# A function table set loaded by hand ahead of each logarithm group of a mixer on ScalarE

## The chip, the cores and the metric

The kernel runs on one core of one Trainium2 chip. The metric is the device time of one execution in microseconds (us); the time given for a kernel is the median of several executions. A core has five engines that run their own queues in order and wait for each other through semaphores: TensorE (PE in the profile, with its weight loads as PEld), VectorE (DVE), ScalarE (ACT), GpSimd (POOL) and SyncE (SP), which here issues most of the transfers.

## What is computed

A decoder trunk of two layers over 1024 tokens of width 1024, float32. The first layer mixes by eight retention heads and eight RWKV-7 heads side by side, the second by sliding-window attention; each is followed by a SwiGLU feed-forward, and a last RMS norm ends the trunk. What matters here is the first layer's mixer, cut to its lines with a nonlinear function:

```python
n = rms_norm(h, norm1_g[0]); z = n @ w_in                      # rsqrt
q, k, v, g = split(z_ret); o = chunk_retention(rotary(q), rotary(k), v)
ret_out = head_group_norm(o) * silu(g)                          # rsqrt, silu
w_log = -softplus(-(w0 + tanh(wl) @ w_up)) - 0.5
decay = exp(-exp(w_log));  a = sigmoid(a0 + al @ a_up)
gate = sigmoid(gl) @ g_up
kk = kkf / maximum(norm(kkf), 1e-12)                            # rsqrt
y = rwkv7_scan(r, decay, k * (1 + (a - 1) * k_a), v, -kk, kk * a)
rwkv_out = (head_group_norm(y) * ln_g + ln_b + bonus) * gate    # rsqrt
out = concat(ret_out, rwkv_out) @ w_out
```

## The kernel before

The tokens are worked in two halves of 512, features on the 128 partitions. Matmuls of the projections are split into a high and a low part and run as three products. ScalarE has no reciprocal square root in use: each `rsqrt` is a logarithm followed by an exponential with scale -0.5, two instructions on ScalarE. Sigmoid, silu and the decay are written with Tanh and Exp in the mixer; the feed-forward uses Silu.

An activation on ScalarE needs its function in the table set that is loaded. Unless the kernel loads a set by name, a load is put in ahead of an activation whose function is not in the set that stands; it appears in the profile as `ACT_TABLE_LOAD` with the line of that activation.

The mixer (`mixer0`) writes its instructions through a planner (`Plan`): chains of work, written as Python generators, and projection jobs (`step`, the line of all mixer matmuls is L240) are drawn in the order of an estimated time that the planner keeps. Its chains are

- `first_norm` and `second_norm`: the RMS factor of each half. `factor` (L479 logarithm, L480 exponential) belongs to the first, L566 and L567 to the second.
- `pair`, eight times (two halves, four pairs of heads): Tanh for decay and a (L685, L687), the decay's running sum by a scan on VectorE (L690), the norm of the key (sum of squares by a matmul, L695 maximum on VectorE, L696 logarithm, L697 exponential), decay factors (L699, L700), then products on VectorE (L705 to L717) and small matmuls.
- `unit`, four times (each two pairs): a triangular inverse on VectorE (L850, L854), transposes (L877), the recurrence over eight chunks (matmul, then L952 on VectorE), and the group norm of two outputs: two logarithms (L980), two exponentials (L982).
- `ret`, eight times (two halves, four pairs of retention heads): scores, state, and the group norm (L1116 logarithm, L1117 exponential), whose result is multiplied on VectorE (L1118) and GpSimd (L1119) by the gate.

The evacuation of a projection holds further Tanh calls: L647 and L650 for the two low-rank inputs, L1025 for the retention gate. ScalarE also makes the high part of each weight tile (L335) and many copies out of PSUM (L776, L783, L890, L902, L914 and others); these and the squares need no table of their own.

What the chains write is one instruction stream per engine. It is compiled with a scheduler on, which may issue an engine's instructions in another order than written where data allow it. `keep` ties one instruction behind the one written last before it on the same engine, without a wait for its end. At the end of the trunk the kernel already loads the set `natural_log_exp_and_others` by name and ties it with `keep` (L1817); `final_r` (L1668 to L1674) follows.

After the mixer, `rstd` (L374 logarithm, L375 exponential) makes the RMS factors of the other norms, six times; the first two calls stand at the start of the first feed-forward (`factor_of`), ahead of its first Silu (L1237).

## Time and profile before

| what | value |
|---|---|
| median of 3 executions | 2348.12 us (2346.57 to 2348.34) |
| the profiled execution, its own time | 2351.35 us |
| its span, from the first to the last instruction | 2349.6 us |
| mean granted TensorE clock | 0.991 |
| ScalarE instructions | 1953 |
| DMA | 407.46 MB, mean 173 GB/s |

The profile comes from one execution, so sums are made against 2351.35 us, and a difference is then carried to the median. Busy time is that of instructions at work; PE's includes modelled ends of pipelined matmuls. A row of a group reads: line, engine, operation, output and inputs, count, then busy time in us and mean ns of one, then the idle time of the engine just before these instructions with what ended it. A row of the timeline reads: start in us, duration, engine, line, operation, output and inputs, count, and in brackets the idle time before it and its releaser. L240 and L335 are lines of helpers that many parts share.

### The profile page before, as it was taken

The page shows a single profiled execution, that of the slowest core. Times are in us where ns is not written, and L with a number is a line of the kernel's source. Part 1 is how long each engine was busy: PE and PEld are TensorE (multiplying, and loading weights), DVE is VectorE, ACT ScalarE, POOL GpSimd, SP SyncE. Part 2 cuts the span into 40 slices and gives each one's busy share as a digit, 9 for nine tenths or more (in the row PEclk, how much of TensorE's full clock was granted, in tenths as well). Part 3 has the DMA queues.
Part 4 walks back from the last instruction along what each step waited for, and adds up shares of the span by engine and source line. Part 5 has one row for each costly group of instructions (what it writes and reads, how often), then busy time and mean ns, then how long its engine had stood idle before and what let it go on. Part 6 is the DMA issues. An engine that isn't in the chain of part 4 may idle for free.

```text
span 2349.6 us, 35675 instructions
## 1 busy us (share of the span) xinstructions
PE 2301.8 (98%) x13056; PEld 1822.8 (78%) x13056; DVE 1703.8 (73%) x2667; ACT 1055.7 (45%) x1953; POOL 976.7 (42%) x764
## 2 busy tenths in 40 slices
PE   8999999999999999999999999999999999999998
PEld 6777777777777888888788887777688888887886
DVE  6876765866557548888876876887747788888767
ACT  5354533323555433333333455666735333333335
POOL 3122121211343057777677600002201677776775
PEclk9999999999999999999999999999999999999999
DMA  7565554443345645665685332123236566556763
GB/s 274 199 208 178 180 156 133 131 126 115 126 166 173 208 156 201 216 217 199 231 299 202 126 119 73 51 69 112 93 114 227 172 210 220 212 202 256 257 215 112
DMA packets 170622, 407.46 MB, mean 173 GB/s; under 512 B 43216, under 2 KB 45904, under 8 KB 170448
## 3 DMA queue, kind: packets, MB, share of 16 engines
q1 hardware_dynamic: 167040, 398.63, 49.5%
q10 hardware_dynamic: 2832, 4.45, 0.5%
q8 instruction: 104, 1.70, 0.3%
q0 software_dynamic: 576, 2.10, 0.2%
q14 instruction: 70, 0.57, 0.1%
HBM read 276.53 MB, written 123.21 MB: 170 GB/s over the span
## 4 chain that ended last, share of the span: by engine, by line
PE 75%; DVE 10%; ACT 4%; DMA 4%; issue 4%; POOL 2%; SPq 1%; DVEq 0%; ACTq 0%; POOLq 0%
PE ps_m L1182 7%; PE ps_m L1184 7%; PE ps_m L1183 7%; PE ps_f L240 7%; PE ps_m L240 5%; PE ps_f L350 4%; PE ps_f L352 4%; PE ps_f L351 4%; PE ps_f L1184 4%; PE ps_f L1183 4%; PE ps_f L1182 4%; PE ps_r L1182 2%; PE ps_r L1184 2%; PE ps_r L1183 2%; PE ps_c L1184 2%
## 5 line engine op out<-in xcount | busy, mean ns | idle before, releaser
L240 PE MATMUL ps_f<-n,w 128*128 128x512 f32 x1440 | 387.1, 416 | 10.4 <-ACT w L335 5.7
L240 PEld LDWEIGHTS ps_f<-n,w 128*128 128x128 f32 x1440 | 269.8, 193 | 95.3 <-issue 24.6
L336 POOL TENSOR_TENSOR w<-wr,w 128x512 fp32r<-128x512 f32 x63 | 86.7, 1384 | 524.3 <-ACT w L335 520.6
L335 ACT CAST w<-wr 128x512 fp32r<-128x512 f32 x231 | 141.1, 617 | 181.2 <-PE ps_f L352 70.3
L336 DVE TENSOR_TENSOR w<-wr,w 128x512 fp32r<-128x512 f32 x168 | 119.9, 717 | 56.8 <-ACT w L335 56.3
L336 POOL TENSOR_TENSOR w<-wq,w 128x512 fp32r<-128x512 f32 x91 | 130.4, 1444 | 31.4 <-ACT w L335 31.4
L1182 PE MATMUL ps_m<-n,w 128*128 128x512 f32 x333 | 130.7, 393 | 0.0
L1184 PE MATMUL ps_m<-n,w 128*128 128x512 f32 x333 | 129.8, 390 | 0.4 <-POOL w L1370 0.4
L1183 PE MATMUL ps_m<-n,w 128*128 128x512 f32 x333 | 129.6, 389 | 0.0
L352 PE MATMUL ps_f<-n,w 128*128 128x512 f32 x320 | 126.9, 397 | 0.6 <-POOL w L336 0.6
L350 PE MATMUL ps_f<-n,w 128*128 128x512 f32 x320 | 127.3, 399 | 0.1
L351 PE MATMUL ps_f<-n,w 128*128 128x512 f32 x320 | 126.9, 396 | 0.0
L1191 DVE TENSOR_TENSOR nq<-ps_m,u 128x512 f32<-128x512 f32 x88 | 58.8, 683 | 92.2 <-PE ps_m L1184 92.1
L1182 PE MATMUL ps_f<-n,w 128*128 128x512 f32 x287 | 113.9, 397 | 1.6 <-ACT u L1341 1.6
L1184 PE MATMUL ps_f<-n,w 128*128 128x512 f32 x287 | 112.1, 392 | 0.0
L1183 PE MATMUL ps_f<-n,w 128*128 128x512 f32 x287 | 111.8, 389 | 0.0
L358 POOL TENSOR_TENSOR n<-nq,n 128x512 fp32r<-128x512 f32 x60 | 100.0, 1679 | 7.6 <-ACT n L356 7.6
L1370 POOL TENSOR_TENSOR w<-wd,w 128x512 fp32r<-128x512 f32 (+1 forms) x62 | 85.9, 1393 | 39.6 <-ACT w L1369 37.9
L1182 PE MATMUL ps_m<-cb,w 128*128 128x512 f32 x236 | 91.9, 390 | 0.3 <-DVE nq L1191 0.3
L1183 PE MATMUL ps_m<-cb,w 128*128 128x512 f32 x236 | 91.8, 389 | 0.0
L1184 PE MATMUL ps_m<-cb,w 128*128 128x512 f32 x236 | 91.8, 389 | 0.0
L1370 POOL TENSOR_TENSOR w<-ws,w 128x512 fp32r<-128x512 f32 (+1 forms) x48 | 71.3, 1491 | 47.0 <-ACT w L1369 43.5
(520 smaller groups left out, 6472.9 us busy)
## 6 DMA issues: line engine op xcount, KB each, us to landing
hc<-n SPq DMA_DIRECT2D x84, 512.0 KB, 2.9
wsp<-w SPq DMA_DIRECT2D x54, 512.0 KB, 3.4
w<-wsp SPq DMA_DIRECT2D x54, 512.0 KB, 3.7
n<-hc SPq DMA_DIRECT2D x54, 512.0 KB, 5.7
wq<-in_w_gate SPq DMA_DIRECT2D x44, 512.0 KB, 4.4
u<-u SPq DMA_DIRECT2D x88, 256.0 KB, 2.9
wr<-in_w_in SPq DMA_DIRECT2D x34, 512.0 KB, 5.2
ha<-hc SPq DMA_DIRECT2D x34, 512.0 KB, 5.6
```

Of the source, the lines that this page charges most:

```text
L240: self.nc.tensor.matmul(out, lhsT, rhs, **kw)
L335: nc.scalar.copy(hi[:, :n], raw[:, c])
L336: self.lo.tensor_tensor(out=lo[:, :n], in0=raw[:, c], in1=hi.bitcast(F32)[:, :n], op=ALU.subtract)
L350: nc.tensor.matmul(ps, hi, rh, start=k == 0, stop=False)
L351: nc.tensor.matmul(ps, hi, rl, start=False, stop=False)
L352: nc.tensor.matmul(ps, lo, rh, start=False, stop=k == n - 1)
L358: e.tensor_tensor(out=lo, in0=src, in1=hi.bitcast(F32), op=ALU.subtract)
L1182: mm(ps, hi, xh, start=first and k == 0, stop=False, skip_group_check=True)
L1183: mm(ps, hi, xl, start=False, stop=False, skip_group_check=True)
L1184: mm(ps, lo, xh, start=False, stop=last and k == len(w) - 1, skip_group_check=True)
L1191: self.last_add = V.tensor_tensor(out=o, in0=x, in1=y, op=ALU.add)
L1370: nc.gpsimd.tensor_tensor(out=lo, in0=v, in1=hi.bitcast(F32), op=ALU.subtract)
```

## The change

Ahead of each logarithm group of the mixer, the set that serves both logarithm and exponential is loaded by name, tied behind the ScalarE instruction written last before it. There are five places: `factor`, `second_norm`, `pair`, `unit` (once for its two logarithms) and `ret`. Nothing else is touched; `rstd` and the tail are as before.

```diff
@@ def factor
         nc = self.nc
+        self.lnexp()
         r = self.rs = self.t(self.mp, [P, HT], "rs", 2)
         nc.scalar.activation(r, ps, AF.Ln, bias=self.cst["eps"][:, 0:1])
         nc.scalar.activation(r, r, AF.Exp, scale=-0.5)
@@ behind keep
+    def lnexp(self):
+
+        self.keep(self.nc.scalar.preload_act_table_set("natural_log_exp_and_others"))
@@ def second_norm
         r = self.t(self.mp, [P, HT], "rs", 2)
+        self.lnexp()
         nc.scalar.activation(r, ps, AF.Ln, bias=self.cst["eps"][:, 0:1])
@@ def pair
         V.tensor_scalar(out=rn, in0=ps, scalar1=1e-24, scalar2=None, op0=ALU.max)
+        self.lnexp()
         S.activation(rn, rn, AF.Ln)
         S.activation(rn, rn, AF.Exp, scale=-0.5)
@@ def unit
+        self.lnexp()
         for y, q in ys:
             ps = self.pst("m", [P, HT])
             self.mm(ps, self.cst["blk"], q, start=True, stop=True)
             S.activation(q, ps, AF.Ln, scale=1.0 / 64, bias=self.cst["eps"][:, 2:3])
@@ def ret
         self.mm(ps, self.cst["blk"], o, start=True, stop=True)
+        self.lnexp()
         S.activation(o, ps, AF.Ln, scale=1.0 / 64, bias=self.cst["eps"][:, 1:2])
         S.activation(o, o, AF.Exp, scale=-0.5, bias=self.cst["eps"][:, 3:4])
```

## The prediction

> **What bounds the kernel now.** I read the page first, then a table of stretches, the groups of ScalarE (ACT), the waits, and last the timeline around each place where TensorE (PE) stood idle.

> ```profile
> PE 2301.8 (98%) x13056; PEld 1822.8 (78%) x13056; DVE 1703.8 (73%) x2667; ACT 1055.7 (45%) x1953; POOL 976.7 (42%) x764
> ...
> PE 75%; DVE 10%; ACT 4%; DMA 4%; issue 4%; POOL 2%; SPq 1%; DVEq 0%; ACTq 0%; POOLq 0%
> ...
> L240 PE MATMUL ps_f<-n,w 128*128 128x512 f32 x1440 | 387.1, 416 | 10.4 <-ACT w L335 5.7
> ...
> L1182 PE MATMUL ps_m<-n,w 128*128 128x512 f32 x333 | 130.7, 393 | 0.0
> ```
> ```profile
> 40.00:690.00 650.00, 630.46 (x5505) 482.06 (x5504) 437.77 (x921) 283.41 (x453) 151.25 (x169) 0.97 0.48 155
> ```

> PE is busy 98% of the span, ScalarE 45%, and ScalarE is 4% of the chain that ended last. The second fence is by stretch: length, then busy time of PE, weight loads, VectorE (DVE), ScalarE and GpSimd. The mixer, where the change acts, is about the first 690 us. From 40 us on PE stands visibly idle for 650 - 630.5 = 19.5 us there. That is the first limit on any gain: ScalarE time counts only where PE waits for it in the end. A softer reserve is that the mixer's projection matmul takes 416 ns against 393 ns for the same shape in the feed-forward; over 1440 of them 33 us, part of it the granted clock of 0.97.

> Next, what switches of the function table cost:

> ```profile
> L696 ACT ACT_TABLE_LOAD x8 | 10.3, 1283 | 0.1
> L697 ACT ACT_TABLE_LOAD x8 | 10.3, 1283 | 0.1
> L1116 ACT ACT_TABLE_LOAD x8 | 10.3, 1283 | 0.1
> L1117 ACT ACT_TABLE_LOAD x8 | 10.3, 1283 | 0.1
> L980 ACT ACT_TABLE_LOAD x8 | 10.3, 1283 | 0.1
> L982 ACT ACT_TABLE_LOAD x8 | 10.3, 1283 | 0.1
> ...
> L374 ACT ACT_TABLE_LOAD x6 | 7.7, 1283 | 0.1
> L375 ACT ACT_TABLE_LOAD x6 | 7.7, 1283 | 0.1
> ...
> L479 ACT ACT_TABLE_LOAD x1 | 1.3, 1283 | 0.0
> ...
> L567 ACT ACT_TABLE_LOAD x1 | 1.3, 1283 | 0.0
> ```

> Each logarithm of the mixer has a load ahead of it and each exponential behind it another: 6 x 8, and 4 single ones from L479 to L567 (L480 and L566 lie between), are 52 loads, 66.7 us of ScalarE. No such row exists for the Tanh lines (L647, L650, L685, L687, L1025): what the exponential loads serves Tanh too, so Tanh comes free now.

> **What goes.** A load by hand for a logarithm and its exponential is in the kernel already, at its end:

> ```profile
> 2304.59 1.28 ACT L1817 ACT_TABLE_LOAD   x1
> ...
> 2328.59 0.67 ACT L1668 ACTIVATE y<-ps_m,c_eps 128x512 f32<-128x512 f32 x1
> 2329.29 0.63 ACT L1670 ACTIVATE y<-y 128x512 f32<-128x512 f32 x1
> ```

> Logarithm (L1668) and exponential (L1670) follow without a load between. So the 26 second loads of the mixer (8 + 8 + 8 + 2, lines L697, L1117, L982, L480, L567) go, 26 x 1.283 = 33.4 us of ScalarE, and the 26 first ones become 22 by hand (a unit's two logarithms share one). The set also stays for the next two logarithms outside (L374 at 687 and 733 us), which lose both loads: four more. What that is worth to PE I read at its idle places:

> ```profile
> 83.95 0.27 PE L240 MATMUL ps_m<-c_ident,AR 64*64 64x64 f32 x2 [1.38 <-DVE GG L769]
> ...
> 170.27 1.28 ACT L697 ACT_TABLE_LOAD   x1
> ...
> 173.82 0.48 PE L240 MATMUL ps_m<-UV,GG 128*64 128x64 f32 x4 [2.01 <-DVE UV L915]
> ...
> 209.63 0.75 DVE L705 SCALAR_TENSOR_TENSOR rt<-rkk,pv,rt 128x512 f32<-128x512 f32 x1 [4.66 <-ACT rt L697]
> ...
> 211.23 0.48 PE L240 MATMUL ps_m<-AR,GT 64*64 64x64 f32 x4 [2.24 <-DVE GT L952]
> ...
> 455.33 1.28 ACT L1117 ACT_TABLE_LOAD   x1
> ...
> 459.31 1.28 ACT L697 ACT_TABLE_LOAD   x1
> ...
> 461.27 0.75 DVE L705 SCALAR_TENSOR_TENSOR rt<-rkk,pv,rt 128x512 f32<-128x512 f32 x1 [3.02 <-ACT rt L697]
> ...
> 469.64 0.69 PE L240 MATMUL ps_c<-TZ,GG 32*32 32x32 f32 x30 [1.46 <-DVE TZ L877]
> ...
> 735.25 1.28 ACT L375 ACT_TABLE_LOAD   x1
> ...
> 745.45 0.50 PE L1182 MATMUL ps_f<-n,w 128*128 128x512 f32 x1 [1.58 <-ACT u L1341]
> ```

> Brackets give the idle time before an instruction and what ended it. At 170 us the load holds ScalarE's copy L914, that holds DVE's L915, and PE waits 2.01 us: 1.28 come back. At 207 us a load of L697 holds L705 at the head of DVE's queue, the recurrence step L952 stands behind it, and PE waits 2.24: 1.28. At 455 us two loads hold L705 in the same way; the transposes behind it cost PE 1.46 here and 1.46 in two shorter waits before it (an estimate of 2.5 back). At 735 us both loads of L374/L375 go, and PE waits 1.58 for what follows: 1.58. At 84 us PE waits 1.38 for DVE, in whose queue L705 had waited for the L697 of that pair: at most 1.28. At the start:

> ```profile
> 22.40 1.14 ACT L335 CAST w<-wr 128x512 fp32r<-128x512 f32 x2 [4.89 <-DMA wr<-in_w_in]
> ...
> 28.26 2.11 PE L240 MATMUL ps_f<-n,w 128*128 128x512 f32 x8 [0.72 <-DVE z L640]
> ```

> The new load, which waits for no data, fits into the 4.89 us in front of the cast; the two old ones stand between this cast and L640, so the 0.72 us for which PE waits go. Sum: 1.28 + 1.28 + 2.5 + 1.58 + 1.28 + 0.72 = **8.6 us**. Without the piece at 735 us that is 7.0 of the 33.4 us taken off ScalarE in the mixer: about a fifth (0.21) reaches PE. I use this fifth for what I can't place. First loads: 4 fewer, 5.1 us, a fifth is **1.1 us** gained.

> **What is added.** Wherever Tanh follows a logarithm group, the table with Tanh must come back.

> ```profile
> 33.34 0.63 ACT L647 ACTIVATE wa<-wa 64x512 f32<-64x512 f32 x1
> ...
> 51.30 1.28 ACT L696 ACT_TABLE_LOAD   x1
> 54.47 0.63 ACT L696 ACTIVATE rt<-rt 128x512 f32<-128x512 f32 x1 [1.89 <-DVE rt L695]
> ...
> 99.21 0.63 ACT L1025 ACTIVATE r<-r 128x512 f32<-128x512 f32 x1 [2.23 <-DMA DT<-dn]
> ...
> 609.28 0.63 ACT L1025 ACTIVATE r<-r 128x512 f32<-128x512 f32 x1 [0.33 <-POOL w L336]
> ```

> In ScalarE's order of time Tanh follows a logarithm group 15 times, from 33.34 to 609.28 us: 15 x 1.283 = 19.2 us. A load runs ahead of its instruction's wait (the load of L696 at 51.30, its logarithm, after a wait of 1.89, at 54.47), so a wait of 1.3 us or more in front of the Tanh, as the 2.23 at 99.21, hides it. I count 8 such and 7 with less (the last, with 0.33, is one): 9.0 us exposed. Their price is not in the trace, since Tanh pays nothing now. The bounds are 0 (all in slack) and 9.0 (all reach PE); the nearest row is the fifth of the loads removed: **1.9 us** lost. Where the cover of the 8 is gone, 10.3 us more come to ScalarE, 2 at that rate.

> **Where the new load lands.** keep ties it behind the ScalarE instruction written last before it, not the logarithm behind the load, and instructions do not run as written:

> ```profile
> 48.24 0.63 ACT L699 ACTIVATE rt<-rt 128x512 f32<-128x512 f32 x1 [1.19 <-DVE rt L690]
> ...
> 401.96 0.63 ACT L1025 ACTIVATE r<-r 128x512 f32<-128x512 f32 x1 [2.19 <-DVE r L1023]
> 402.61 1.28 ACT L980 ACT_TABLE_LOAD   x1
> ```

> L699 is written behind L696 and runs ahead of it (48.24 against 54.47); at 401.96 a Tanh runs between the two logarithms of one unit. Where a Tanh comes between, or the logarithm overtakes the load, its two loads stay and the one by hand is waste. The load itself waits for no data, so nothing queues behind a wait, only behind its 1.28 us. Bounds: no misfire, or all 22. I take 3, from the crowded stretch of 316 to 406 us; each costs about two loads more than a group that works, 7.7 us, a fifth is **1.6 us**.

> **The sum**: -8.6 - 1.1 + 1.9 + 1.6 = **-6.2 us**. The loads of mixer and of the two L374 groups fall from 56 to some 37 without misfires, 43 with three. Against the profiled execution's own 2351.35 us (span 2349.6) this is 2345.2; that execution lies 3.2 us above the median of 2348.12, so I forecast 2341.9, rounded to 2342.

> [...] Each load takes 1283 ns in the rows, the eight of L697 have 0.1 us of idle before them in all, and the one at 402.61 starts 0.02 us after the Tanh before it ended. [...]

> [...]

> **Rivals.**
> - *The returns eat most of it* (**0.21**). For it: 7 returns stand without cover, most on L685 and L687, the head of a pair's chain, whose VectorE queue already waits for ScalarE at L688. At twice the fifth, returns and misfires cost 7.0 and 2.7 of the 9.7 us gained are left: 2345.4.
> - *It does not do what it says* (**0.10**): so many loads by hand are overtaken that the number stays near 56. Each misfire gives back two loads of 19, so this takes 9 or 10 of the 22. Against it: between most first loads and their logarithm nothing runs. Time: 2348.
> - *Slower* (**0.17**): each exposed return delays L688 and with it the decay scan L690, at the head of VectorE's queue (busy 437.8 of 650 us there), and this reaches PE in full. Then 9.0 + 7.7 = 16.7 us are lost against 9.7 gained: +7.0, 2355.1. It turns to a loss when over 58% of the added load time reaches PE, and shows as slower from 86%. Against it: of the removed loads, in the same queues, only a fifth did.
> - *More than forecast* (**0.10**): stalls hidden in the 416 ns matmuls shrink as well; if 15 of the 19.5 us visible and 33 hidden go, 2333.

> **How the numbers follow.** The forecast has 0.42. A measurement of this kernel tells about 0.2% (4.7 us) from no change. Faster: 0.42 + 0.10 = 0.52. Same: 0.21 + 0.10 = 0.31. Slower: 0.17. The range takes in the larger gain and reaches to the slower rival's price: 2333 to 2356. The forecast's own range is 2336 to 2343.4.

> **What would show it.** Right: no loads at L697, L1117, L982, L480 and L567, but at L685, L647 and L1025; the idle of PE in front of ps_m<-UV,GG, ps_m<-AR,GT and ps_c<-TZ,GG down by 1 to 3 us each; DVE's wait at L705 shorter by about one load in each of the 8 pairs, that at L688 longer; the mixer's end earlier by 4 to 6 us and the feed-forward as long as before. Wrong: loads still at L696 or L1116 beside those by hand, or PE's idle in the mixer not below 19 us, or a difference that arises after 760 us, where the change puts nothing.

## The result: 17 us faster, about three times the forecast

The changed kernel takes 2331.62 us (median of 6 runs, 2328.36 to 2336.31) against 2348.67 us (6 runs, 2346.57 to 2349.74): a ratio of 0.9927, 95% interval 0.9916 to 0.9938. The forecast was 2342.0 us, with 2333 as its lower end. The sign was right, the size was not.

**The profile after.** The profiled execution took 2330.62 us (span 2328.6, before 2349.6). In the changed kernel a line number stands 1 to 9 higher than before: L697 is now L704, L685 L691, L688 L694, L705 L712, L980 L988, L1025 L1033, L1116 L1125; L494 is the load by hand. First from the page, then the mixer's stretch (its columns as before: length, busy time of PE, weight loads, VectorE, ScalarE and GpSimd, then the granted clock):

```profile
PE 2289.3 (98%) x13056; PEld 1816.4 (78%) x13056; DVE 1704.2 (73%) x2667; ACT 1044.2 (45%) x1943; POOL 979.8 (42%) x764
...
PE 69%; DVE 5%; ACT 2%; issue 1%; POOL 0%; DMA 0%; DVEq 0%; POOLq 0%; ACTq 0%
...
L240 PE MATMUL ps_f<-n,w 128*128 128x512 f32 x1440 | 379.3, 411 | 8.9 <-ACT w L335 5.7
```
```profile
40.00:690.00 650.00, 636.19 (x5579) 489.53 (x5578) 454.43 (x940) 284.78 (x463) 162.92 (x173) 0.99 0.51 164
```

PE's idle time between 40 and 690 us fell from 19.5 to 13.8 us, the mean clock there rose from 0.97 to 0.99, and the same 1440 projection matmuls take 411 ns in place of 416. The groups of table loads:

```profile
L494 ACT ACT_TABLE_LOAD x22 | 28.2, 1283 | 0.4
L1033 ACT ACT_TABLE_LOAD x8 | 10.3, 1283 | 15.1 <-issue 8.5 <-DVE r L1031 6.6
...
L691 ACT ACT_TABLE_LOAD x5 | 6.4, 1283 | 2.4 <-PE ps_m L240 2.4
...
L1125 ACT ACT_TABLE_LOAD x2 | 2.6, 1283 | 0.0
L1126 ACT ACT_TABLE_LOAD x2 | 2.6, 1283 | 0.0
L988 ACT ACT_TABLE_LOAD x2 | 2.6, 1283 | 0.0
L990 ACT ACT_TABLE_LOAD x2 | 2.6, 1283 | 0.0
...
L653 ACT ACT_TABLE_LOAD x1 | 1.3, 1283 | 0.0
L703 ACT ACT_TABLE_LOAD x1 | 1.3, 1283 | 0.0
L704 ACT ACT_TABLE_LOAD x1 | 1.3, 1283 | 0.0
```

There are 22 loads by hand, 14 returns (8 for the retention gate's Tanh, 5 for a pair's, 1 for L653), and 10 loads at five logarithms that their load by hand missed (four groups, one of them a unit with two logarithms). With those 46 in the mixer, and no load left at the two L374 groups that end it, the whole kernel has 65 loads, 75 before.

Where the time arose: the first logarithm and the second of the norm behind the mixer, in the changed kernel, then before.

```profile
670.44 0.69 ACT L374 ACTIVATE rs<-ps_m,c_eps 128x512 f32<-128x512 f32 x1 [1.54 <-PE ps_m L373]
...
713.64 0.69 ACT L374 ACTIVATE rs<-ps_c,c_eps 128x512 f32<-128x512 f32 x1
```
```profile
688.61 0.69 ACT L374 ACTIVATE rs<-ps_m,c_eps 128x512 f32<-128x512 f32 x1 [0.18 <-PE ps_m L373]
...
734.54 0.69 ACT L374 ACTIVATE rs<-ps_c,c_eps 128x512 f32<-128x512 f32 x1
```

They are 18.2 and 20.9 us earlier. From the second to the end of the span it is 1614.93 us after and 1615.04 before: the whole gain lies ahead of 735 us. But PE's visible idle time over the whole span fell only from 47.76 to 39.23 us, by 8.5 of the 21.0. The other 12 are in the granted clock. These are stretches of before on a grid of 3.41 us, and the number behind the five engines is the clock:

```profile
170.26:173.67 3.41, 1.55 (x22) 1.00 (x20) 1.83 (x4) 2.87 (x5) 0.00 (x0) 1.00 0.15 59
173.67:177.08 3.41, 3.26 (x31) 2.81 (x32) 3.32 (x8) 1.29 (x4) 0.00 (x0) 0.50 0.00 0
207.80:211.22 3.42, 1.20 (x36) 0.99 (x32) 1.59 (x4) 2.78 (x4) 0.00 (x0) 1.00 0.18 69
211.22:214.63 3.41, 3.40 (x46) 2.93 (x47) 3.41 (x9) 0.62 (x1) 0.00 (x0) 0.50 0.37 154
214.63:218.04 3.41, 3.41 (x15) 2.70 (x14) 0.86 (x2) 0.00 (x0) 0.00 (x0) 0.50 0.00 0
```

These are two of the places from which the prediction worked. PE is idle 1.86 us of the first stretch, and in the next one the clock is half; 2.22 us of the third, and two stretches at half follow, in which PE is busy throughout (3.40 and 3.41 us). Reckoned from the clock of 0.50, such a stretch costs half of its 3.41 us: 1.7 us of matmul time that no idle time shows. In the one from 1166.95 us the 128x512 matmuls start every 0.43 us (1167.33 to 1169.89, six steps), just ahead of it every 0.23 us (1166.01 to 1166.71, three). Before has 11 of them (18.8 us), all from 80 to 1171 us, after has 4 (6.8 us); the tail behind 2300 us, where PE runs out of work, is left out. The difference is the missing 12.

### The profile page after: what moved, and what is told of

It reads as the page before. It is cut to its first block, busy times and chain, and to the rows that moved or that the text cites. A ratio compares the mean times of both kernels' runs of the same rounds, so it can differ in the third digit from the quotient of the medians.

```text
span 2328.6 us, 35662 instructions
## 1 busy us (share of the span) xinstructions
PE 2289.3 (98%) x13056; PEld 1816.4 (78%) x13056; DVE 1704.2 (73%) x2667; ACT 1044.2 (45%) x1943; POOL 979.8 (42%) x764
## 4 chain that ended last, share of the span: by engine, by line
PE 69%; DVE 5%; ACT 2%; issue 1%; POOL 0%; DMA 0%; DVEq 0%; POOLq 0%; ACTq 0%
PE ps_m L1191 7%; PE ps_m L1192 7%; PE ps_m L1193 7%; PE ps_f L350 4%; PE ps_f L351 4%; PE ps_f L352 4%; PE ps_f L1191 4%; PE ps_f L1193 4%; PE ps_f L1192 4%; PE ps_r L1191 2%; PE ps_r L1193 2%; PE ps_r L1192 2%; PE ps_c L1193 2%; PE ps_c L1192 2%; PE ps_c L1191 2%; PE ps_m L240 2%
## 5 line engine op out<-in xcount | busy, mean ns | idle before, releaser
L240 PE MATMUL ps_f<-n,w 128*128 128x512 f32 x1440 | 379.3, 411 | 8.9 <-ACT w L335 5.7
L240 PEld LDWEIGHTS ps_f<-n,w 128*128 128x128 f32 x1440 | 266.6, 190 | 91.4 <-issue 21.8
L336 POOL TENSOR_TENSOR w<-wr,w 128x512 fp32r<-128x512 f32 x63 | 85.9, 1368 | 523.9 <-ACT w L335 520.1
L335 ACT CAST w<-wr 128x512 fp32r<-128x512 f32 x231 | 142.1, 619 | 178.0 <-PE ps_f L352 76.7
L336 DVE TENSOR_TENSOR w<-wr,w 128x512 fp32r<-128x512 f32 x168 | 120.7, 722 | 68.2 <-ACT w L335 67.9
L336 POOL TENSOR_TENSOR w<-wq,w 128x512 fp32r<-128x512 f32 x91 | 130.3, 1442 | 31.9 <-ACT w L335 31.9
```

Source lines behind the costliest of these rows:

```text
L240: self.nc.tensor.matmul(out, lhsT, rhs, **kw)
L335: nc.scalar.copy(hi[:, :n], raw[:, c])
L336: self.lo.tensor_tensor(out=lo[:, :n], in0=raw[:, c], in1=hi.bitcast(F32)[:, :n], op=ALU.subtract)
```

## The experiments

Two theories. **LOADS**: the loads taken off ScalarE's chain make the gain. **ORDER**: the scheduler places instructions by the times that it reckons, loads included, so the change gives another order on every engine, and that makes the gain. Kernels can keep either: loads that are put in or taken out once the order is fixed move nothing else (in the traces the order of ScalarE, VectorE and GpSimd is the same in every place, TensorE's in all but 8 or fewer of 13056).

**e1: the order of after with the loads of before** (75 loads).

```
+    for b in nc.main_func.blocks:      # after scheduling
...
+            if type(i).__name__ == "InstLoadActFuncSet" and n < 22:
+                n += 1
+                continue
```

> The instruction order of the changed kernel on every engine, but without its 22 loads by hand: each logarithm and each exponential gets its own load again, 75 in all as before the change. Theory LOADS (the gain is table-load time taken out of ScalarE's queue, which ends idle time of TensorE and the half-clock stretches behind it): back near the time before, 2343 to 2353 us. Rival ORDER (the gain comes from the other instruction order that the scheduler found): stays near the changed kernel, 2330 to 2337 us.

Measured: 2341.53 us (2337.53 to 2344.08), ratio 0.997 (0.9959 to 0.9981). Between the two.

**e2: the order of before with loads by hand** (44 loads: 18 of the joint set, each directly ahead of a logarithm that needs it, so none misses). This reaches further than the change: two of the 18 serve the four later L374 groups, and six of the 31 loads saved lie there, behind 1300 us; e3 has the same.

```
+            if f == "Ln" and not loaded and k < 24:
+                res.append(left.pop(0))
```

> The instruction order of the kernel before on every engine, with 18 loads of the joint set put in directly ahead of those logarithms that need one, after scheduling: 44 loads in all instead of 75, none misplaced. LOADS: 2326 to 2336 us, with granted clock in the mixer near 0.99. ORDER: 2345 to 2350 us.

Measured: 2339.43 us (2338.09 to 2342.73), ratio 0.9962 (0.995 to 0.9975). Between the two again: neither theory alone.

**e3: the order of after with each load directly ahead of its logarithm** (both edits above; 44 loads).

> The instruction order of the changed kernel, with its 22 loads by hand taken out after scheduling and 18 put back directly ahead of the logarithms that need one: 44 loads in all instead of 65. LOADS: each load still in the way counts, so 3 to 8 us below the changed kernel, 2323 to 2329 us. ORDER: no change against it, 2330 to 2334 us.

Measured: 2326.23 us (2324.47 to 2330.99), ratio 0.9905 (0.9891 to 0.9919), as LOADS had it. This is the fastest version, 5.4 us under the median of the changed kernel, though the two intervals overlap a little.

What the two factors are worth is clearer from all runs of each kernel, with each run's span split in two: span x granted clock is reckoned as the span at full clock, the rest as lost to the clock (means; one run's clock has three digits, 2.3 us to the last one, so only the means bear on this). The part lost to the clock holds 2.5 to 4.2 us of the tail, where PE has no work, in every profiled execution.

| kernel | order | loads | runs | clock | lost to clock | span at full clock |
|---|---|---|---|---|---|---|
| before | old | 75 | 36 | 0.9921 | 18.7 | 2328.8 |
| e2 | old | 44 | 5 | 0.9930 | 16.4 | 2321.8 |
| e1 | new | 75 | 7 | 0.9949 | 12.0 | 2327.7 |
| after | new | 65 | 6 | 0.9960 | 9.3 | 2320.6 |
| e3 | new | 44 | 5 | 0.9960 | 9.3 | 2315.9 |

From before over e1 to after, the order gives 1.1 us at full clock and 6.7 of clock, and then the loads 7.1 at full clock and 2.7 of clock: together 8.2 us of waits and 9.4 us of clock, 17.6 us between the means. In the clock the two add up (with 44 loads on both sides, e2 to e3, the order gives 7.1, and the loads give 2.3 and 2.7). A mean's standard error in the column of the clock is 0.4 us for before and 0.7 to 1.5 for the others, so the order's part is clear of noise and the loads' part of 2.3 to 2.7 is not, or hardly. At full clock, with standard errors of 0.3 to 0.9 us, they do not add up: 31 loads fewer give 7.0 in the old order and 11.8 in the new one, and the order's 1.1 by itself is hardly clear of noise. The rows for the mixer show the new order with the old loads (e1) and with 44 (e3):

```profile
40.00:690.00 650.00, 630.11 (x5555) 484.12 (x5555) 446.13 (x933) 291.70 (x465) 157.66 (x171) 0.99 0.50 163
```
```profile
40.00:690.00 650.00, 637.65 (x5581) 490.84 (x5580) 455.62 (x940) 265.47 (x448) 163.95 (x173) 0.99 0.51 164
```

With before's loads PE is idle 19.9 us, as before (19.5), yet the clock is 0.99, not 0.97; with 44 loads it is idle 12.35.

**e4: more work on ScalarE in the feed-forward.** In the changed kernel the copy L1350 is done 11 times at 8 places, to make PE stand idle there.

```
-        self.nc.scalar.copy(u0, ps)
+        for _ in range(11 if self.nearly in range(4, 20, 2) else 1):
+            self.nc.scalar.copy(u0, ps)
```

> The changed kernel with a delay of known size where nothing else stalls: at 8 places of the first feed-forward ScalarE's copy out of PSUM is done 11 times instead of once (the same values), about 4.8 us, so that TensorE has to wait some 2 to 3 us at each. If a wait of TensorE costs only its own length: the time grows by the visible idle, some 16 to 24 us, and the granted clock there stays 1.0. If each wait is followed by a stretch at half clock, as the rows of the kernel before suggest (0.5 for 3.4 us or 6.8 us behind idles of 2 us): 14 to 27 us more than the idle, and a granted clock of 0.8 to 0.9 there.

Measured: 2338.57 us (2334.06 to 2341.31), ratio 0.9955 (0.9941 to 0.9968). It missed its purpose: the scheduler put other work between the copies, and PE stood idle only 2.9 us more from 690 to 830 us, at a clock of 1.00. It says little on the clock. Of the 6.9 us over the changed kernel, PE's idle time from 690 to 1350 us accounts for 3.7; the rest stays open. All engines keep the order of the changed kernel up to 735 us.

**e5: pauses of known length, order fixed.** The same question, put in after scheduling.

```
+        g.append(nc.scalar.preload_act_table_set(sets[k % 2]).ins)   # n times
+        g.append(nc.scalar.copy(pad[k], one).ins)
...
+        if i.engine == mybir.EngineType.Activation and "Silu" in str(getattr(i, "func", "")):
+            if n in at:
+                res += made[list(at).index(n)]
```

> The changed kernel, all instructions in its order, with 16 pauses put on ScalarE in the two feed-forwards, each directly ahead of a SiLU: 2, 3, 4, 5, 6, 7, 8 or 10 table loads (alternating between two sets, a copy of one column between them), once each in either feed-forward. A pause is about n x (1.28 + 0.2) + 1.28 us, 4 to 16 us. No other load or order is touched, and the clock of the changed kernel is 1.00 there. CLOCK theory (a visible idle of TensorE of some 2 us brings a stretch of half clock behind it): idles under 1.2 us leave the clock at 1.0; behind those of 2 us and more the 3.4 us windows show 0.5 for 3.4 or 6.8 us, so the 20 us windows fall to 0.91 or 0.83, and the time grows by the added idle and 1.7 to 3.4 us more for each such place. IDLE theory (half clock comes by chance, not from idle): the clock stays 1.00 from 700 to 2100 us whatever the idle, and the time grows by the added idle alone.

Measured: 2444.83 us (2 runs, 2444.69 and 2444.97), ratio 1.041 (1.039 to 1.0431), 113.2 us above the changed kernel. Between the two profiled executions the span grew by 114.1 us and PE's idle time by 79.8; the other 34.3 have no idle time to stand for them. Three pairs of neighbouring stretches:

```profile
953.12:956.53 3.41, 2.24 (x10) 1.57 (x10) 3.38 (x4) 1.98 (x4) 3.03 (x3) 1.00 0.28 86
956.53:959.95 3.42, 2.54 (x12) 1.74 (x10) 3.38 (x3) 1.74 (x4) 3.42 (x3) 1.00 0.51 184
1212.55:1215.96 3.41, 1.27 (x4) 0.47 (x3) 3.41 (x5) 0.27 (x2) 1.42 (x1) 1.00 1.03 402
1215.96:1219.37 3.41, 2.95 (x7) 2.37 (x8) 3.41 (x5) 0.54 (x2) 1.61 (x1) 0.50 1.04 421
...
922.41:925.82 3.41, 0.00 (x0) 0.00 (x0) 3.38 (x3) 0.62 (x1) 3.41 (x3) 1.00 0.37 154
925.82:929.23 3.41, 1.29 (x3) 1.13 (x4) 3.41 (x5) 0.81 (x2) 0.82 (x1) 0.50 0.00 0
```

An idle of 1.17 us left the next stretch at full clock, 2.14 us brought half, and so did a whole idle stretch. Between 700 and 2300 us half clock fills 92 us here and 3.4 us in the changed kernel. So CLOCK holds and IDLE falls: half clock came behind the pauses of PE. Of the 92 us PE was busy in 67.4, and half of that, 33.7 us, is by the same reckoning the matmul time lost there (1.6 us in the changed kernel): that is nearly all of the 34.3.

**e6, e7 and e8: other orders, with the loads of before.** Is another order better in itself, or only this one? First the two low-rank matmuls at the head of a pair swapped, then the planner's cost of a pair's first step at 8.0 and at 9.5 in place of 8.5:

```
-        self.mm(ps, self.wua[0:64, pc], self.wa[0:64, :], start=True, stop=True)
         self.mm(ps2, self.wua[64:128, pc], self.wa[64:128, :], start=True, stop=True)
+        self.mm(ps, self.wua[0:64, pc], self.wa[0:64, :], start=True, stop=True)
```
```
-        yield (), 8.5
+        yield (), 8.0        # and 9.5
```

> The kernel before, its 75 loads untouched; only the two LoRA matmuls at the head of a pair are written in the other order (a few hundred places of TensorE's order change, nothing else is added or taken). CHANCE theory (any other order of the same work moves the time by several us either way, by idle and half-clock stretches): outside 2346 to 2350, or close to it, since the order changes little: 2340 to 2356. SPECIFIC theory (the order of the changed kernel is better because the scheduler placed work by the shorter loads; orders are otherwise alike): 2346 to 2350.

> The kernel before, its 75 loads untouched; only the cost that the planner is told for the first step of a pair is 8.0 in place of 8.5, which gives another order on every engine (about a sixth as many places on TensorE as the change moved). CHANCE theory: off the 2348 by 3 to 10 us, in either direction, with idle and granted clock both changed. SPECIFIC theory: 2346 to 2350.

> As the run before, the cost being 9.5 in place of 8.5. CHANCE theory: off the 2348 by 3 to 10 us, in either direction, and not by the same amount as with 8.0. SPECIFIC theory: 2346 to 2350.

Measured: 2347.6 us (2344.24 to 2357.16), ratio 1.0002 (0.9988 to 1.0015); 2349.42 us (2344.9 to 2356.01), 1.0004 (0.9992 to 1.0016); 2343.84 us (2338.8 to 2348.41), 0.9978 (0.9967 to 0.9989). In the traces TensorE's order differs from that of before in 339, 2616 and 1957 of its 13056 places (in 1369 for the change), so e7 moved twice as many as the change, not a sixth as was expected. Split as in the table (10 runs each): lost to clock 18.8, 17.9 and 11.0 us, at full clock 2328.6, 2330.4 and 2330.6; the 25 runs of before on the same chip have 18.8 and 2329.1. Two of three orders leave the time where it was, as SPECIFIC had it; the third, which does not touch a load, gains as much clock as the order of the changed kernel does (7.8 against 6.7 us) and pays 1.5 us of it back in waits. This is what CHANCE had for it. So the clock part belongs to the order as such, can be had without the change, and is not in every order. Whether the order of the changed kernel has it by luck or because it was laid for fewer loads stays open: three orders are too few.

## Why the prediction was wrong, step by step

- **The step that failed** is the first: "That is the first limit on any gain: ScalarE time counts only where PE waits for it in the end", and with it the working that gives 1.28 us for a load behind an idle of PE. An idle of 2 us in this kernel costs its own length and, where 1.8 us or more of it lie in one stretch of the 3.41 us grid (58 of 59 such were followed by half clock, as the last section has it), another 1.7 us or 3.4 us, reckoned from one or two stretches at 0.50 behind it. The clock makes 9.4 of the 17.6 us between the means: 6.7 of them came with the new order, 2.7, not clear of noise, with the loads. The granted clock of 0.97 stood in the prediction as "a softer reserve" and entered no term. Windows of 3.41 us at the idle places would have shown it in the trace of before.
- **The second loads, -8.6**, were near as waits, in sum: the whole change, with returns and misfires, was to give 6.2 us and gives 8.2 at full clock. By place, PE's groups, before and then after:

```profile
L240 PE MATMUL ps_m<-UV,GG 64*64 64x64 f32 (+1 forms) x512 | 19.1, 226 | 2.0 <-DVE UV L915 2.0
...
L240 PE MATMUL ps_m<-AR,GT 64*64 64x64 f32 x256 | 15.3, 234 | 2.2 <-DVE GT L952 2.2
L240 PE MATMUL ps_m<-c_ident,AR 64*64 64x64 f32 x256 | 9.2, 221 | 1.4 <-DVE GG L769 1.4
...
L240 PE MATMUL ps_c<-TZ,GG 32*32 32x32 f32 x256 | 6.2, 192 | 3.3 <-DVE TZ L877 3.2
```
```profile
L240 PE MATMUL ps_m<-UV,GG 64*64 64x64 f32 (+1 forms) x512 | 18.7, 223 | 0.7 <-DVE UV L819 0.4 <-DVE UV L922 0.3
...
L240 PE MATMUL ps_m<-AR,GT 64*64 64x64 f32 x256 | 15.5, 224 | 2.0 <-DVE GT L959 2.0
L250 PE MATMUL ps_m<-c_ident,r 128*128 128x128 f32 x64 | 9.2, 274 | 1.9 <-DVE XA L933 1.1 <-issue 0.8
L240 PE MATMUL ps_m<-c_ident,AR 64*64 64x64 f32 x256 | 9.2, 221 | 1.2 <-DVE GG L776 1.1
L240 PE MATMUL ps_c<-TZ,GG 32*32 32x32 f32 x256 | 6.1, 192 | 0.4 <-DVE TZ L884 0.4
```

  The last figures are the idle time in front of the group. UV,GG gave 1.3 (1.28 forecast) and TZ,GG 2.9 (2.5); AR,GT and the place at 84 us gave 0.2 each (1.28 each), and 1.9 new ones stand in front of the transposes of r. From 690 to 760 us PE is now busy 70.00 of 70.00 us, so the 1.58 us behind L374 came back whole; from 0 to 40 us its idle time fell by 0.9 (0.72). These are 7.1 of the 8.6, less the 1.9. At AR,GT the second load is gone, but VectorE now runs L336, L712, L715 and L716 ahead of the recurrence step L959, where L705 and L336 stood before, so the new order filled the place.
- **The queue** behind the logarithm moved as foreseen. VectorE at L705 and L688 before, at the same two after:

```profile
L705 DVE SCALAR_TENSOR_TENSOR rt<-rkk,pv,rt 128x512 f32<-128x512 f32 x8 | 6.0, 751 | 18.9 <-ACT rt L697 18.9
L688 DVE TENSOR_SCALAR rt<-rt 128x512 f32<-128x512 f32 x8 | 3.9, 490 | 6.7 <-ACT rt L685 6.7
```
```profile
L712 DVE SCALAR_TENSOR_TENSOR rt<-rkk,pv,rt 128x512 f32<-128x512 f32 x8 | 6.8, 855 | 4.6 <-ACT rt L704 4.4
L694 DVE TENSOR_SCALAR rt<-rt 128x512 f32<-128x512 f32 x8 | 5.8, 721 | 7.4 <-ACT rt L691 7.3
```

  The wait for the exponential fell by 14.3 us over 8 pairs, 1.8 a pair and so more than one load; the one for Tanh grew by 0.7 in all. With it falls the premise of the *slower* rival, that each exposed return would delay this instruction.
- **The fifth** (0.21) was right in the order from which it was read and wrong in the new one. In the old order 31 loads fewer, 39.8 us of ScalarE, gave 7.0 us at full clock: 0.18. In the new order the same 31 gave 11.8: 0.30, and the first 10 of them (e1 to after, 12.8 us) 7.1: 0.55. That an order laid for fewer loads has less room for them would fit, but is not shown.
- **Returns**: 14, not 15, and what was to hide them did not. The prediction took it from L696 that a load runs ahead of its instruction's wait, and so counted 8 of 15 as hidden. At six of the 14 the wait of 0.4 to 8.5 us stands in front of the load, and the Tanh follows at once:

```profile
248.26 1.28 ACT L1033 ACT_TABLE_LOAD   x1 [3.94 <-DVE r L1031]
249.56 0.63 ACT L1033 ACTIVATE r<-r 128x512 f32<-128x512 f32 x1
```

  Only the load at L653 lies wholly in front of a longer wait (3.3 us). The price of the returns was not measured by itself; it is within the 8.2 us.
- **Misfires**: four groups with five logarithms and 10 loads, not three with 6, so 46 loads, not 43. Besides, nine of the 22 loads by hand serve no logarithm that lacked the set: five find it loaded already, four are followed by another load before a logarithm comes. With each load directly ahead of its logarithm the span at full clock is 4.7 us shorter (e3 against after, 21 loads or 26.9 us of ScalarE less). Six of the 21 lie behind the mixer, where e3's profiled execution is 1.1 us shorter, so not all of the 4.7 need be the mixer's. 1.6 us for three was too little; the 26.9 us count at 0.17, so what was too small is the number of loads that misses and idle loads bring, not the rate.
- **The lower end of the forecast's own range**, 2336 us, lies 4.4 us from the result, but no run shows a term that leads to it. It asks for about twice the 6.2 us of the sum, while a load took 1283 ns in every row, and in front of the 22 of L494 ScalarE stood idle for 0.4 us in all.
- **What the prediction left out** is that the change moves the order on all engines: 1369 of 13056 places on TensorE, 391 of 2667 on VectorE, 70 of 1878 on ScalarE without the loads, 24 of 764 on GpSimd. That the scheduler does so because it reckons the time of the loads is argued, not shown. It was treated as a change of ScalarE alone. This is worth 1.1 us at full clock and 6.7 of clock.
- **The rivals**: *more than forecast* (0.10, 2333 us) came nearest, and its mechanism is partly right. The 1440 projection matmuls take 7.8 us less in sum (387.1 to 379.3), but by half-clock stretches in them, not by hidden stalls: outside these stretches one takes 410.2 ns before and 409.4 after. Of the signs, the waits in front of UV,GG and TZ,GG fell as named and that of AR,GT did not, and loads at L696, L1116 and L980 beside those by hand, a sign of being wrong, came in five cases; "the mixer's end earlier by 4 to 6 us" failed (18 to 21); "the feed-forward as long as before" held.

## What to carry to other kernels

Price an idle of the matmul engine with the clock behind it: lay 3.4 us windows over every idle above 1 us, and count half a window, 1.7 us, more for each that is followed by half clock (an estimate from the clock of 0.50, and shown here for one kernel). Where a scheduler orders the program, a change of one engine's durations is also a change of the order; hold the order fixed, with the old durations and with the new, before the gain is put down to either. And place a table load by hand directly ahead of the call that needs it, after the order is known, if it can be done.

## What the runs showed of the hardware

```profile
174.45 0.68 PE L240 MATMUL ps_m<-UV,GG 128*64 128x64 f32 x14 [1.96 <-DVE UV L922]
```
```profile
169.74:173.16 3.42, 2.75 (x29) 1.89 (x25) 0.75 (x2) 3.34 (x6) 0.00 (x0) 1.00 0.21 85
173.16:176.57 3.41, 2.12 (x32) 1.84 (x33) 3.33 (x7) 1.52 (x4) 0.00 (x0) 1.00 0.00 0
176.57:179.98 3.41, 3.41 (x28) 2.54 (x27) 3.38 (x7) 0.99 (x2) 2.08 (x1) 1.00 0.06 24
```

The 1.96 us are cut by the grid, 0.67 in the first window and 1.29 in the second, and the clock stays full. By these numbers an idle of about 2 us is estimated to cost 2 us or nearly 4 (2 + 1.7; more where two stretches follow), by where the grid falls. The places change from one execution to the next: up to 690 us the kernels after, e4 and e5 run the same loads in the same order, and half clock starts at 207, 289 and 593 us in the first, at 83, 210 and 462 in the second, at 291 and 591 (two stretches) in the third. That would also fit the scatter of one kernel's runs (before, 25 runs on one chip: 2344.93 to 2354.06 us), but the cost is three stretches in each of the three, so that the grid makes this scatter is not shown.

All 75 table loads of before and all 65 of after take 1283 ns each. The 22 loads of L494 have 0.4 us of idle in front of them in all, and the 90 loads of e5, which alternate between two sets, 1283 ns each on average and 0.6 us of idle in front of them in all, with 1.0 us in all in front of the copies behind them.
